# The first feed-forward stage begun on the scale alone, its shift added to four column chunks afterwards

## The chip, the cores and the metric

One core of a Trainium2 chip runs the whole kernel. Five engines work side by side, each through its own queue of instructions in order: TensorE (PE, matmuls and transposes), VectorE (DVE), ScalarE (ACT), GpSimd (POOL, here almost only the issuing of DMAs) and SyncE (SP, DMAs). The metric is the device time of one execution in microseconds (us).

## The reference, cut to what matters

Two layers, 384 tokens (128 of context, 256 latent), width 1024. Only the beginning of layer 0 is touched:

```python
mod = jax.nn.silu(cond) @ p["w_ada"] + p["b_ada"]          # one vector for context, one for latent tokens
mod = mod.reshape(cond.shape[0], N_MOD, 1, D_MODEL)        # (shift, scale, gate) x 3 for each layer
h = rmsnorm(x, g[0]) * (1.0 + mod[:, 1]) + mod[:, 0]       # scale is mod 1, shift is mod 0
x = x + 0.5 * mod[:, 2] * swiglu(h, p["w_ffn_in"][0], p["w_ffn_out"][0])
...                                                       # mixer, then a second such FFN
def swiglu(h, w_in, w_out):
    g, u = jnp.split(h @ w_in, 2, axis=-1)
    return (jax.nn.silu(g) * u) @ w_out
```

With r the factor of the norm for a token, `h @ w_in` is r * ((x * scale') @ w_in) + shift @ w_in, so the shift can be added behind the matmul. The kernel uses that before and after the change.

## The kernel before, in words

Everything is kept with features on the partitions: `xT` is 8 blocks (k = 0 to 7) of 128 features by 384 tokens. Each product is made of three matmuls (`mm3`: wh*xh, wh*xl, wl*xh), for which ACT rounds an operand to its upper part (`wh`, `rH`, `hH`, `aH`) and DVE subtracts it to get the rest (`wl`, `rL`, `hL`, `aL`).

Six stages follow one another: FFN, mixer, FFN for each of two layers. In an FFN the 2816 hidden columns are worked in 22 chunks f; a chunk is 24 matmuls for gate (`pg`) and 24 for up (`pu`), three for each block k, then SiLU, product and split; then 8 output blocks (`po`). The weights of a chunk come in two halves q (k 0 to 3 and 4 to 7), loaded by SP into tiles `X` (5 buffers) and split into `H` and `L` (4 buffers each, so two chunks).

The modulation vectors of 18 groups (stage s; p = shift, scale, gate) are products of `sc` (SiLU of the conditions) with slices of `w_ada`. POOL loads them, 512 KB at a time, into `AX` (3 buffers), and the stream `ada` works them in steps of one block k: on DVE (two instructions over 1024 columns into `accs`, then at the group's end eight matmuls with ones, `adaps`), or on PE (`adaps<-adax,sc`). The numbers in `ADA_F` and `ADA_M` say how many steps stand in each stage.

At the start shift and scale of the first FFN are made apart from that stream: `ada_first(i)`, i = 0 to 3, loads 256 columns of each of the two (four tiles of 512 KB, by SP) and makes 32-row matmuls into one bank, a copy by ACT (`adasb`), a transpose (`psada`) and two small DVE instructions (`md`, `am`). Then `raw_chunk` makes x * scale' for two blocks k, with the shift as two further columns. So the first two chunks of the FFN (`N_RAW`) can start on blocks 0 and 1 while w_ada is still loading. Their banks hold 386 columns, the last two being shift @ w_in, which SiLU and product add. From chunk 2 on the FFN uses `hs`, the fully modulated x (`mod_chunk`).

The order on each engine is made by the framework's scheduler from dependencies and priorities (`ahead`, `placed`); `behind` adds an order without a wait. `late_loads` issues 17 small parameter loads on POOL (among them `gains` and `rot`) once the last `raw_chunk` is done.

Of the kernel before, what the change touches and what calls it, by code (L numbers as in the profile page):

```python
# [84 lines left out]
def hybrid_step_kernel(  # L85
# [104 lines left out]
    mm = nc.tensor.matmul  # L190
    V = nc.vector
# [105 lines left out]
    def ada_first(i):  # L297
# [3 lines left out]
        for q in range(2):  # L301
            xs = []
            for g in range(2):
                if (i + q) % 2 == 0:
                    x = kp.tile([P, HALF_K, 256], F32, name="adax", tag="K")
                else:
                    x = wp.tile([P, HALF_K, 256], F32, name="adax", tag="X")
                rows = w_ada[0, q * HALF_K * P : (q + 1) * HALF_K * P, g * D + 256 * i : g * D + 256 * i + 256]
                nc.sync.dma_start(x, rows.rearrange("(k p) n -> p k n", p=P))
                xs.append(x)  # L310
            for kk in range(HALF_K):
                k = q * HALF_K + kk
                for g in range(2):
                    for j in range(2):
                        r0 = 64 * g + 32 * j
                        mm(
                            bank[r0 : r0 + 32, 0:P],
                            sc[:, k, :],
                            xs[g][:, kk, j * P : (j + 1) * P],
                            start=(k == 0),  # L320
                            stop=(k == KD - 1),
                        )
# [20 lines left out]
    def ada_group(s, p, on_dve):  # L343

        l, i = divmod(s, 3)
# [3 lines left out]
        bias = vC[l][:, i * 24 + KD * p : i * 24 + KD * p + KD]  # L349
        accs = [K5(f"ada{c}") for c in range(2)] if on_dve else None  # L350
        bank = None if on_dve else PS("adaps", "pa")
        for k in range(KD):
            x = wp.tile([P, 1024], F32, name="adax", tag="AX", bufs=3)
            nc.gpsimd.dma_start(x, w_ada[l, k * P : (k + 1) * P, c0 : c0 + D])  # L354
            if on_dve:
                x = x.rearrange("p (h n) -> p h n", h=2)
# [8 lines left out]
            else:  # L365
                x = x.rearrange("p (m a j) -> p a m j", m=KD, a=4)
                for a in range(4):
                    ins = mm(bank[32 * a : 32 * a + 32, 0:256], sc[:, k, :], x[:, a], start=(k == 0), stop=(k == KD - 1))
# [960 lines left out]
    for i in range(4):  # L1329
        ada_first(i)  # L1330
        for k in (2 * i, 2 * i + 1):
            raw_chunk(0, k)
# [61 lines left out]
```

## Time and profile before

| | us |
|---|---|
| median of 3 runs | 1578.61 (1577.85 to 1579.18) |
| the profiled execution, its own time | 1580.6 |
| its span, first to last instruction | 1578.8 |
| first matmul of the first FFN begins | 22.54 |
| its chunk 2 begins (the two raw chunks are done) | 58.58 |
| its output blocks begin | 230.27 |
| first mixer's scores begin | 439.07 |
| second FFN's first matmul | 523.61 |

The times in the stretch are counted from the span's start. In what follows "the start" is the stretch to 58.58 us.

### The profile page before, as it was taken

What the parts mean: (1) busy time and instruction counts of PE and PEld (TensorE: products, weight loads), DVE (VectorE), ACT (ScalarE), POOL (GpSimd) and SP (SyncE); (2) the same over time, 40 slices, a digit from 0 to 9 for tenths busy, and PEclk for the clock granted to TensorE, in tenths of its full rate; (3) what the DMA queues carried; (4) which work ended last, traced back from release to release, by engine and by line L of the source; (5) the groups of instructions that cost most, each with busy time, mean ns of one, the idle gap of its engine ahead of it and who ended that gap; (6) DMA issues with size and microseconds to landing.
All of it is one profiled execution on the core that took longest, in us unless ns stands there. A gap on an engine that the chain in (4) does not pass through costs nothing.

```text
span 1578.8 us, 24260 instructions
## 1 busy us (share of the span) xinstructions
PE 1527.9 (97%) x9118; PEld 1441.2 (91%) x9118; DVE 1113.6 (71%) x2068; ACT 746.6 (47%) x1376; POOL 103.4 (7%) x194
## 2 busy tenths in 40 slices
PE   7999999999889999999999999999978999999998
PEld 5899999998668999999999999999857699999998
DVE  5888586587677988578578866777967789443332
ACT  4533332469577633333363333325975864333221
POOL 1202010001100001001000200110000000000000
PEclk9999999999999999999999999999989999999999
DMA  9978576523531587566537866674231046444341
GB/s 304 248 205 228 158 231 196 147 80 115 185 106 37 146 245 211 161 207 225 171 97 215 238 187 193 203 238 121 64 92 37 15 134 201 130 117 128 116 145 35
DMA packets 291034, 249.02 MB, mean 158 GB/s; under 512 B 11554, under 2 KB 273159, under 8 KB 290917
## 3 DMA queue, kind: packets, MB, share of 16 engines
q1 hardware_dynamic: 270224, 175.94, 38.2%
q0 software_dynamic: 20368, 71.34, 14.8%
q8 instruction: 71, 1.16, 0.3%
q14 instruction: 47, 0.38, 0.1%
q10 hardware_dynamic: 324, 0.20, 0.1%
HBM read 245.17 MB, written 2.27 MB: 157 GB/s over the span
## 4 chain that ended last, share of the span: by engine, by line
PE 88%; DVE 4%; ACT 4%; issue 2%; DMA 1%; POOL 0%; ACTq 0%; DVEq 0%; POOLq 0%
PE po L475 9%; PE po L476 9%; PE po L477 9%; PE pg L475 8%; PE pg L477 8%; PE pg L476 8%; PE pu L475 8%; PE pu L477 8%; PE pu L476 8%; PE psw L476 1%; PE psg L891 1%; PE psw L475 1%; PE psw L477 1%; PE adaps L378 1%; ACT gate L143 1%
## 5 line engine op out<-in xcount | busy, mean ns | idle before, releaser
L471 DVE TENSOR_TENSOR wl<-wx,wh 128x1024 fp32r<-128x1024 f32 (+2 forms) x332 | 385.4, 1163 | 302.8 <-ACT wh L470 294.3
L470 ACT CAST wh<-wx 128x1024 fp32r<-128x1024 f32 (+2 forms) x332 | 333.2, 1005 | 448.5 <-PE po L476 237.3
L362 DVE SCALAR_TENSOR_TENSOR ada<-adax,sc,ada 128x1024 f32<-128x1024 f32 x196 | 244.2, 1280 | 17.8 <-DMA adax<-in_w_ada_dram 17.4
L475 PE MATMUL po<-aH,wh 128*128 128x384 f32 x704 | 239.7, 341 | 0.0
L477 PE MATMUL po<-aH,wl 128*128 128x384 f32 x704 | 237.7, 338 | 0.0
L476 PE MATMUL po<-aL,wh 128*128 128x384 f32 x704 | 237.2, 337 | 0.0
L475 PE MATMUL pg<-hH,wh 128*128 128x384 f32 x640 | 216.9, 339 | 0.0
L475 PE MATMUL pu<-hH,wh 128*128 128x384 f32 x640 | 216.2, 338 | 0.0
L477 PE MATMUL pg<-hH,wl 128*128 128x384 f32 x640 | 215.9, 337 | 0.2 <-DVE wl L471 0.2
L477 PE MATMUL pu<-hH,wl 128*128 128x384 f32 x640 | 215.6, 337 | 0.0
L476 PE MATMUL pu<-hL,wh 128*128 128x384 f32 x640 | 215.5, 337 | 0.0
L476 PE MATMUL pg<-hL,wh 128*128 128x384 f32 x640 | 215.4, 337 | 0.0
L143 ACT ACTIVATE sg<-pg 128x384 f32<-128x384 f32 x80 | 39.4, 493 | 206.5 <-PE pg L477 206.5
L475 PEld LDWEIGHTS po<-aH,wh 128*128 128x128 f32 x704 | 132.4, 188 | 3.9 <-issue 2.1
L476 PEld LDWEIGHTS po<-aL,wh 128*128 128x128 f32 x704 | 132.2, 188 | 0.5 <-issue 0.5
L477 PEld LDWEIGHTS po<-aH,wl 128*128 128x128 f32 x704 | 132.2, 188 | 0.0
L354 POOL DMA_DIRECT2D adax<-in_w_ada_dram x128 | 68.1, 533 | 892.3 <-DVE ada L360 466.5
L475 PEld LDWEIGHTS pg<-hH,wh 128*128 128x128 f32 x640 | 120.2, 188 | 2.5 <-issue 2.1
L477 PEld LDWEIGHTS pg<-hH,wl 128*128 128x128 f32 x640 | 120.1, 188 | 0.6 <-DVE wl L471 0.5
L476 PEld LDWEIGHTS pg<-hL,wh 128*128 128x128 f32 x640 | 120.2, 188 | 0.0
L475 PEld LDWEIGHTS pu<-hH,wh 128*128 128x128 f32 x640 | 120.2, 188 | 0.0
L477 PEld LDWEIGHTS pu<-hH,wl 128*128 128x128 f32 x640 | 120.1, 188 | 0.0
(327 smaller groups left out, 2425.9 us busy)
## 6 DMA issues: line engine op xcount, KB each, us to landing
wx<-in_w_ffn_in_dram SPq DMA_DIRECT2D x352, 256.0 KB, 4.1
adax<-in_w_ada_dram POOLq DMA_DIRECT2D x128, 512.0 KB, 4.9
wx<-in_w_ffn_out_dram SPq DMA_DIRECT2D x80, 512.0 KB, 3.9
wx<-in_w_in_dram SPq DMA_DIRECT2D x28, 512.0 KB, 3.8
adax<-in_w_ada_dram SPq DMA_DIRECT2D x16, 512.0 KB, 7.7
wx<-in_w_ffn_out_dram SPq DMA_DIRECT2D x16, 256.0 KB, 3.3
wx<-in_w_out_dram SPq DMA_DIRECT2D x8, 512.0 KB, 3.9
wx<-in_w_out_dram SPq DMA_DIRECT2D x16, 256.0 KB, 2.7
```

Source lines behind the costliest of these rows:

```text
L143: ins = nc.scalar.activation(out, in_, func, **kw)
L354: nc.gpsimd.dma_start(x, w_ada[l, k * P : (k + 1) * P, c0 : c0 + D])
L362: ins = V.scalar_tensor_tensor(accs[c], x, w, accs[c], ALU.mult, ALU.add)
L378: mm(bank[32 * a : 32 * a + 32, 256 * c : 256 * c + 256], cm(C_ONE, n1=32), x[:, a], start=True, stop=True)
L470: nc.scalar.copy(h[:, 0:nk, 0:ncol], x[:, 0:nk, 0:ncol])
L471: V.tensor_tensor(lo[:, 0:nk, 0:ncol], x[:, 0:nk, 0:ncol], h[:, 0:nk, 0:ncol].bitcast(F32), ALU.subtract)
L475: mm(out, wh, xh, start=first, stop=False)
L476: mm(out, wh, xl, start=False, stop=False)
L477: last_mm[0] = mm(out, wl, xh, start=False, stop=last)
L891: mm(ps[:, 0:TG], wg[:, wi, :], xcs[ch], start=True, stop=True)
```

## The change: what it does

At the start only the scale is loaded and made (`scale_load`, `scale_first`; matmuls of two 32-row groups in place of four). The first four chunks (`N_LATE`) are made from x * scale' alone, 384 columns, and kept as r * gate and r * up in SBUF (`late_acts`). The shift becomes an ordinary group (0, 0) of the stream, worked by PE between and inside chunks 2 and 3, with loads in six buffers (three of `K`, three of `AX`); its first load waits for the last scale matmul. The shift's part of the four chunks is a new group (0, 1): the four chunks' columns of `w_ffn_in` are loaded again by POOL (8 times 512 KB) and multiplied by the shift on DVE, and `late_shift` adds the result, does SiLU, product and split. Chunks 4 and 5 are now the ones with 386 columns. `begin` writes out the order; with `strict` on, every engine keeps the order in which the code is written. `ADA_F[0]` goes from 20 to 28 steps, which begin at chunk 6 instead of 2. The matmuls of the stream are put behind the last `mm3` that is written ahead of them (`last_mm`), before behind the norm's (`norm_last["pe"]`), in the mixers too.

```diff
-ADA_F = [[20, 12], None, [24, 12], [20, 16], None, [8, 0]]
+ADA_F = [[28, 12], None, [24, 12], [20, 16], None, [8, 0]]
+N_LATE = 4
...
+            def run(*a, **k):
+                ins = fn(*a, **k)
+                if strict["on"]:
+                    if self.last is not None:
+                        tc.add_manual_dep(ins.ins, self.last, no_sync, reason="order on the engine")
+                    self.last = ins.ins.name
+                return ins
...
+    TE, SC, V = (InOrder(e) for e in (nc.tensor, nc.scalar, nc.vector))
...
+        late = (s, p) == (0, 1)
+        on_dve = on_dve or late
...
+            if (s, p) == (0, 0) and k % 2 == 0:
+                x = kp.tile([P, 1024], F32, name="adax", tag="K")
+            else:
+                x = wp.tile([P, 1024], F32, name="adax", tag="AX", bufs=3)
+            if late:
+                win = w_ffn_in[0, 0, k * P : (k + 1) * P, :].rearrange("p (g n) -> p g n", g=2)
+                nc.gpsimd.dma_start(x.rearrange("p (g n) -> p g n", g=2), win[:, :, 0 : N_LATE * P])
...
-                    w = sc[:, k, c : c + 1]
+                    w = md[:, k, c : c + 1] if late else sc[:, k, c : c + 1]
...
-                    if norm_last["pe"] is not None:
-                        behind(ins, norm_last["pe"])
+                    behind(ins, last_mm[0])
...
-    ada = Stream([(0, 2)] + [(s, p) for s in range(1, 3 * DEPTH) for p in range(3)])
+    ada = Stream([(s, p) for s in range(3 * DEPTH) for p in range(3)])
...
+        scale_first(2, scales[2])
+        raw_chunk(0, 4)
+        raw_chunk(0, 5)
+        part(1, (2, 3))
+        weights(0, 1)
+        part(0, (4, 5))
+        scale_first(3, scales[3])
+        raw_chunk(0, 6)
+        raw_chunk(0, 7)
+        weights(1, 1)
+        part(1, (4, 5))
+        part(0, (6, 7))
+        keep(0)
+        for q in range(2):
+            weights(2, q)
+        part(1, (6, 7))
+        keep(1)
+        for f in range(2, N_LATE):
+            b.append(banks())
+            hidden(b[f][0:1], {q: sl[f, q] for q in range(2)}, raws[0], T)
+            for q in range(2):
+                weights(f + 1, q)
+            ada.step(2 if f == 2 else 4)
+            if f == 3:
+                for k in range(KD):
+                    raw_cols(0, k)
+            hidden(b[f][1:2], {q: sl[f, q] for q in range(2)}, raws[0], T)
+            if f == 2:
+                ada.step(2)
+            keep(f)
+        strict["on"] = False
+        late_loads(norm_last["raw"])
+        hs = [mod_chunk(0, k, r) for k in range(KD)]
...
-            if f >= 2:
+            f0 = first + 2
+            if f >= f0:
```

How the order moves, in three places (rows as the built programs have them; all operations under the recording layer have line L204 in the changed program).

DVE at the very start, before: copies of the transposed x (`xT<-psx`) and the running sum of squares (`acc<-sq`; the squares are ACT's).

```order
L447 COPY xT_112<-psx_113 128x384
L447 COPY xT_112<-psx_120 128x384
L447 COPY xT_112<-psx_128 128x384
L447 COPY xT_112<-psx_136 128x384
L439 SCALAR_TENSOR_TENSOR acc_118<-sq_125,acc_118 128x384
L447 COPY xT_112<-psx_144 128x384
L439 SCALAR_TENSOR_TENSOR acc_118<-sq_133,acc_118 128x384
```

The same place on DVE in the changed program, from the second copy on:

```order
L204 COPY xT_112<-psx_120 128x384
L204 SCALAR_TENSOR_TENSOR acc_118<-sq_125,acc_118 128x384
L204 COPY xT_112<-psx_128 128x384
L204 SCALAR_TENSOR_TENSOR acc_118<-sq_133,acc_118 128x384
L204 COPY xT_112<-psx_136 128x384
L204 SCALAR_TENSOR_TENSOR acc_118<-sq_141,acc_118 128x384
```

Each sum now stands directly behind the copy of its own block; before, the copies ran three blocks ahead.

ACT around the last scale part of the start, before: the copy `adasb` of that part, the cast of a weight half (`wh`), x * scale' of the last two blocks (`rH`).

```order
L324 COPY adasb_445<-ada0_404 128x128
L470 CAST wh_692<-wx_689 128x1024
L143 ACTIVATE rH_451<-xT_112,am_186 128x128
L143 ACTIVATE rH_451<-xT_112,am_186 128x256
L143 ACTIVATE rH_459<-xT_112,am_186 128x128
L143 ACTIVATE rH_459<-xT_112,am_186 128x256
```

The same place on ACT in the changed program; `wh_431` is the second half of chunk 1, `wh_466` the first of chunk 2:

```order
L204 COPY adasb_413<-ada0_396 64x128
L204 ACTIVATE rH_419<-xT_112,am_209 128x128
L204 ACTIVATE rH_419<-xT_112,am_209 128x256
L204 ACTIVATE rH_425<-xT_112,am_209 128x128
L204 ACTIVATE rH_425<-xT_112,am_209 128x256
L204 CAST wh_431<-wx_201 128x1024
L204 CAST wh_466<-wx_463 128x1024
```

The cast of a weight half stands behind the last blocks' rounding now, not ahead of it.

DVE in chunks 3 to 5 of the changed program: `sg_693`, `su_694` are chunk 3's kept halves, `wl_857`, `wl_864` chunk 5's weights, `wl_937` chunk 6's; `tb` are the first mixer's rotary tables.

```order
L204 TENSOR_TENSOR sg_693<-pg_586,y_316 128x384
L204 TENSOR_TENSOR wl_857<-wx_853,wh_856 128x1024
L204 TENSOR_TENSOR su_694<-pu_587,y_316 128x384
L204 TENSOR_TENSOR wl_864<-wx_860,wh_863 128x1024
L204 TENSOR_SCALAR gains_92<-gains_92 128x2x32
L204 COPY rb_838<-pg_787 128x2
L204 TENSOR_SCALAR gains_92<-gains_92 128x2x96
L204 TENSOR_TENSOR tb_2968<-rot_78,gains_92 128x2x32 x4
L204 TENSOR_TENSOR wl_937<-wx_933,wh_936 128x1024
L204 SCALAR_TENSOR_TENSOR hL_716<-ht_714,md_208,hH_715 128x128
L204 SCALAR_TENSOR_TENSOR hL_716<-ht_714,md_208,hH_715 128x256
L204 COPY rb_840<-pu_788 128x2
```

Before, the first of the same `tb` instructions stands behind the eight steps of the stream's first group:

```order
L362 SCALAR_TENSOR_TENSOR ada0_760<-adax_1346,sc_101,ada0_760 128x1024
L362 SCALAR_TENSOR_TENSOR ada1_761<-adax_1346,sc_101,ada1_761 128x1024
L360 TENSOR_SCALAR ada0_1436<-adax_1438,sc_101 128x1024
L683 TENSOR_TENSOR tb_2931<-rot_78,gains_92 128x2x32
L362 SCALAR_TENSOR_TENSOR ada0_1436<-adax_1513,sc_101,ada0_1436 128x1024
```

The tables, which need the late loads of `gains` and `rot`, moved ahead of chunk 6's weights and of all `hL`.

PE in the first mixer, before, from its last compressed-projection matmul (`psc`) on: the stream's matmuls (`adaps`) stand between the transposes and projections.

```order
L981 MATMUL psc<-wl,hH 128x352
L368 MATMUL adaps<-adax,sc 32x256 x18
L989 MATMUL pst<-kc_76,cl 128x128
L368 MATMUL adaps<-adax,sc 32x256 x2
L989 MATMUL pst<-kc_76,cl 128x128
```

PE later in that mixer in the changed program, behind the first output matmuls (`po`), where the scores (`psS`) and the transposes of probabilities (`psT`) begin:

```order
L204 MATMUL adaps<-adax,sc 32x256 x9
L204 MATMUL psS<-kC,qh 128x384
L204 MATMUL adaps<-adax,sc 32x256 x3
L204 MATMUL psS<-kC,qh 128x384
L204 MATMUL pst<-kc_76,stk 96x128 x32
L204 MATMUL adaps<-adax,sc 32x256 x10
L204 MATMUL psS<-kC,qh 128x384
L204 MATMUL psT<-kc_76,prob 128x128
L204 MATMUL adaps<-adax,sc 32x256 x2
```

All 64 matmuls of the stream's two groups moved from ahead of the scores to between them, 42 of them behind the first `psT`, in 17 small bursts.

## Rows read from the trace of the kernel before

**Rows 1.** The page, part 1: busy time, share of the span, instructions.
```profile
PE 1527.9 (97%) x9118; PEld 1441.2 (91%) x9118; DVE 1113.6 (71%) x2068; ACT 746.6 (47%) x1376; POOL 103.4 (7%) x194
```

**Rows 2.** Timeline of PE at the start: start, length, instruction, idle before.
```profile
9.46 1.91 PE L446 MATMUL psx<-kc,xtok 128*128 128x128 f32 x8
...
17.53 2.76 PE L316 MATMUL ada<-adax,sc 128*32 128x128 f32 x60
...
20.97 0.27 PE L326 MATMUL psada<-kc,adasb 128*128 128x128 f32 x1
...
22.54 0.45 PE L475 MATMUL pg<-rH,wh 128*128 128x386 f32 x1
...
58.58 0.34 PE L475 MATMUL pg<-hH,wh 128*128 128x384 f32 x1
58.76 0.34 PE L476 MATMUL pg<-hL,wh 128*128 128x384 f32 x1
```

**Rows 3.** Timeline of ACT at the start.
```profile
16.25 0.49 ACT L143 ACTIVATE sq<-psx 128x384 f32<-128x384 f32 x1 [2.00 <-DVE xT L447]
...
20.34 0.27 ACT L324 COPY adasb<-ada 128x128 f32<-128x128 f32 x1 [1.26 <-PE ada L316]
20.50 1.05 ACT L470 CAST wh<-wx 128x1024 fp32r<-128x1024 f32 x1
21.68 0.80 ACT L143 ACTIVATE rH<-xT,am 128x128 fp32r<-128x128 f32 x2
22.39 1.03 ACT L470 CAST wh<-wx 128x1024 fp32r<-128x1024 f32 x1
```

**Rows 4.** Timeline of DVE at the start.
```profile
15.60 0.56 DVE L447 COPY xT<-psx 128x384 f32<-128x384 f32 x1 [1.48 <-PE psx L446]
16.08 0.55 DVE L439 SCALAR_TENSOR_TENSOR acc<-sq,acc 128x384 f32<-128x384 f32 x1
...
21.56 0.16 DVE L526 CAST rH<-md 128x2 fp32r<-128x2 f32 x1
...
21.86 1.23 DVE L471 TENSOR_TENSOR wl<-wx,wh 128x1024 fp32r<-128x1024 f32 x1
...
44.14 0.74 DVE L512 SCALAR_TENSOR_TENSOR hL<-ht,md,hH 128x128 fp32r<-128x128 f32 x2
44.80 0.74 DVE L508 SCALAR_TENSOR_TENSOR ht<-xT,am,y 128x128 f32<-128x128 f32 x2
```

**Rows 5.** Busy time by stretch: us, each engine's (instructions), granted clock, DMA.
```profile
40.00:44.00 4.00, 1.62 (x12) 0.78 (x13) 3.80 (x9) 3.45 (x8) 0.00 (x0) 0.89 1.09 347
44.00:50.00 6.00, 6.00 (x42) 4.66 (x43) 2.37 (x9) 0.91 (x2) 0.00 (x0) 0.50 1.19 301
...
398.00:403.00 5.00, 1.60 (x26) 0.68 (x24) 5.00 (x8) 4.71 (x10) 1.57 (x3) 1.00 0.72 228
403.00:408.00 5.00, 3.61 (x20) 1.28 (x21) 2.52 (x9) 1.31 (x5) 1.81 (x4) 0.70 1.04 378
...
453.00:487.00 34.00, 30.70 (x206) 21.38 (x205) 27.63 (x101) 30.07 (x104) 0.00 (x0) 1.00 0.10 32
```

**Rows 6.** Timeline of PE: the stream's matmuls after a DVE group.
```profile
127.01 1.07 PE L378 MATMUL adaps<-ada,kc 128*32 128x256 f32 x16
```

**Rows 7.** Timeline of PE: the stream's matmuls in the first mixer.
```profile
398.10 1.50 PE L368 MATMUL adaps<-adax,sc 128*32 128x256 f32 x24
403.27 0.64 PE L368 MATMUL adaps<-adax,sc 128*32 128x256 f32 x8 [3.67 <-DMA adax<-in_w_ada_dram]
```

**Rows 8.** Timeline of POOL: the first late load and that of `rot`.
```profile
55.47 0.59 POOL L226 DMA_DIRECT2D rowsG<-in_diff_subln_dram  x1 [50.79 <-DVE rL L531]
...
60.31 0.57 POOL L226 DMA_DIRECT2D rot<-in_consts_dram  x1
```

**Rows 9.** The tile `rot`: time of its one load.
```profile
DMA to landing us min/median/max: 6.6/6.6/6.6
```

**Rows 10.** The page, part 5: steps of the stream on DVE.
```profile
L362 DVE SCALAR_TENSOR_TENSOR ada<-adax,sc,ada 128x1024 f32<-128x1024 f32 x196 | 244.2, 1280 | 17.8 <-DMA adax<-in_w_ada_dram 17.4
```

More of the change, by code (lines that the diff above doesn't have):

```diff
@@ L188, in small, with __init__, __getattr__ @@
         return const.tile(list(shape), F32, name=name)
-    mm = nc.tensor.matmul
-    V = nc.vector
+    strict = {"on": False}
+    class InOrder:
+        def __init__(self, engine):
+            self.engine, self.last = engine, None
+        def __getattr__(self, name):
+            fn = getattr(self.engine, name)
+            def run(*a, **k):
[5 more added lines that the diff above has]
+                return ins
+            return run
+    TE, SC, V = (InOrder(e) for e in (nc.tensor, nc.scalar, nc.vector))
+    mm = TE.matmul
     kc0 = small("kc0", (P, 2 * P))
@@ L266, in rows_to_cols @@
         ps = PS("psv", "p1")
-        ins = nc.tensor.transpose(ps[:, 0:n], rows[0:n, :], cm(C_ID, 0, n, 0, n))
+        ins = TE.transpose(ps[:, 0:n], rows[0:n, :], cm(C_ID, 0, n, 0, n))
         if after is not None:
@@ L299, in ada_first, with scale_first @@
+    def scale_first(i, xs):
         md, am = new_mods(0)
         bank = PS("ada0", "pa")
[L301 to L322, printed above, removed]
+        for k in range(KD):
+            for j in range(2):
+                ins = mm(
+                    bank[32 * j : 32 * j + 32, 0:P],
+                    sc[:, k, :],
+                    xs[k // HALF_K][:, k % HALF_K, j * P : (j + 1) * P],
+                    start=(k == 0),
+                    stop=(k == KD - 1),
+                )
+        norm_last["scale"] = ins
@@ L352, in ada_group @@
         for k in range(KD):
-            x = wp.tile([P, 1024], F32, name="adax", tag="AX", bufs=3)
-            nc.gpsimd.dma_start(x, w_ada[l, k * P : (k + 1) * P, c0 : c0 + D])
+            if (s, p) == (0, 0) and k % 2 == 0:
+                x = kp.tile([P, 1024], F32, name="adax", tag="K")
+            else:
+                x = wp.tile([P, 1024], F32, name="adax", tag="AX", bufs=3)
+            if late:
+                win = w_ffn_in[0, 0, k * P : (k + 1) * P, :].rearrange("p (g n) -> p g n", g=2)
+                nc.gpsimd.dma_start(x.rearrange("p (g n) -> p g n", g=2), win[:, :, 0 : N_LATE * P])
+            else:
+                ins = nc.gpsimd.dma_start(x, w_ada[l, k * P : (k + 1) * P, c0 : c0 + D])
+                if (s, p) == (0, 0):
+                    if k == 0:
+                        tc.add_manual_dep(ins.ins, norm_last["scale"].ins.name, sync, reason="order of the loads")
+                        first_load.append(ins)
+                    else:
+                        behind(ins, first_load[0])
             if on_dve:
@@ L562, in ffn, with late_shift @@
+    late_acts = []
+    def late_shift(b):
+        for f in range(N_LATE):
+            sg, su_ = late_acts[f]
+            for j, sl in SEG:
+                act(sg[:, sl], sg[:, sl], AF.Silu, bias=b[:, j, 0, f, 0:1])
+            for j, sl in SEG:
+                V.scalar_tensor_tensor(sg[:, sl], su_[:, sl], b[:, j, 1, f, 0:1], sg[:, sl], ALU.add, ALU.mult)
+            late_acts[f] = split(sg, "a", pool=LT)
     def ffn(s, r, hs, last, ready=None):
@@ L797, in cache_prep @@
         pt = PS("pst", "p2")
-        nc.tensor.transpose(pt[:, 0:P], cck[:, 0:P], ident)
+        TE.transpose(pt[:, 0:P], cck[:, 0:P], ident)
         cn = S("cn", (P, P))
-        nc.scalar.copy(cn, pt[:, 0:P])
+        SC.copy(cn, pt[:, 0:P])
         ps = PS("psk", "p2")
@@ L1326, in hybrid_step_kernel @@
     NS = 3 * DEPTH
-    r = norm_stat(0)
-    ready = {0: [], 1: []}
[L1329 to L1332, printed above, removed]
-        if i in (0, 2):
-            for f in range(2):
-                ready[f].append(ffn_slab(0, f, i // 2))
-    hs = [mod_chunk(0, k, r) for k in range(KD)]
-    late_loads(norm_last["raw"])
+    r, hs, ready = begin()
     state_out = small("state_out", (P, 16))
```

182 lines of the change are left out of this document (123 added, 59 removed).

## The prediction

> **What bounds the kernel now.** I read the page first: PE is busy 97% of the span [rows 1], so a change can only bring time where PE waits or works on something that can go. Then the timeline of PE at the start: the first FFN matmul is at 22.54, chunk 2 begins at 58.58, and from there the pitch of a matmul is 58.76 - 58.58 = 0.18 us [rows 2]. Two chunks have 96 matmuls, 96 x 0.176 = 16.9 us; they take 36 us. So the start has some 19 us beside FFN work, and the stretches show where: from 40 to 44 PE is busy 1.62 of 4 us, and from 44 to 50 its granted clock is 0.50, the lower of its two levels (1.2 in place of 2.4 GHz) [rows 5]. That is what the change can attack. From 58.58 on there is next to nothing to win before the first mixer, where PE waits 3.67 us for a stream load [rows 7].
>
> **Start up to chunk 2, worked out along the new order.** Eight of the sixteen first w_ada loads go, 4.2 MB, at the 347 GB/s of [rows 5] 12 us of loading; then the chains between the engines decide.
>
> First the norm's squares. On ACT a square starts only after DVE's copy of its block: copy 15.60 to 16.16, square at 16.25 to 16.74 [rows 3, 4]. The new DVE order puts the sum of a block behind the copy of the same block, so copy, square and sum follow one another: 0.56 + 0.09 + 0.49 + 0.05 + 0.47 (pitch of copy and sum, 16.08 - 15.60 = 0.48) = 1.65 us for each of blocks 2 to 5. The first copy can start near 10.2 (the transposes run from 9.46 at 0.21 us each [rows 2]), block 2 at 12.3, block 5 at 17.3, the last copy ends near 19.9, the last square at 20.5. The scale's copy `adasb` stands behind it on ACT: 20.5, against 20.34 before [rows 3]. Nothing is gained up to here, though PE could be ready at 17.3.
>
> From a copy `adasb` at S, its transpose ends at S + 0.9 and rounding `rH` starts at S + 1.34 (20.97 + 0.27 and 21.68 against 20.34); two blocks of `rH` cost 2 x 0.71 (22.39 - 21.68), a cast 0.95 to 1.05, then `wl` 1.2 [rows 2 to 4]. Followed through the order as written: part 0 at S = 20.5, first FFN matmuls near 24.2 (the second scale copy waits on ACT for cast and `rH` of the first), chunk 0 blocks 0 to 3 until 28.5, the norm's sums 2.3, chunk 1 blocks 0 and 1 until 32.9, scale matmuls 1.5 (32 at 46 ns, from 60 in 2.76 [rows 2]), copy at 34.5, chunk 1 blocks 2 and 3 from 35.5 to 37.6. Then chunk 0 needs its second half, whose cast stands on ACT behind `rH` of blocks 4 and 5 (38.4) and whose `wl` ends at 39.6: PE idles 0.8 twice and ends at 41.4. Last scale part: matmuls to 43.0, `adasb` 43.05, `rH` 44.4 to 45.8, cast to 46.9, `wl` to 48.1. PE has nothing else in between (3.9 us less one transpose), then 10 + 24 matmuls: chunk 2 begins at **54.1**, against 58.58.
>
> This is at full clock. Before, the clock fell after a stretch in which PE was busy 1.62 of 4 us, and 6 us ran at 0.50, 3 us lost; in the mixer a wait of 3.67 us cost 0.30 of 5 us, 1.5 us [rows 5, 7]. The new start has two such stretches: 17.3 to 24.2 (some 2.1 us of work in 7) and 41.4 to 48.1 (some 2). I take 1.8 us for each, nearer the mixer's case: chunk 2 at 57.7, **-0.9 us**. Bounds: no loss (-4.5) and 3 us twice (+1.5).
>
> The Trainium skill, "TensorE: Matmul & The Clock Gate", section on the HAM clock gate, says that the throttled state is the default and activity releases it, so that idling is paid for a second time after it. By that both stretches are paid; by the trace's rows alone one could doubt the second, and the sum would be 1.8 us lower. The trace agrees where it shows the case (granted 0.50 behind the stretch with 1.62 of 4).
>
> **The shift on PE.** 32 matmuls of the program, 64 records of 256 columns, in three bursts of 16, 16 and 32 inside chunks 2 and 3, which had none before. A burst of 16 takes 1.07, one of 24 takes 1.50 [rows 6, 7], so 32 take 1.9: **+4.0 us** (bounds 3.5, if the burst's own ends overlap, and 5). The six buffers hide the loads: the first six are issued near 43 and needed from 58 on; the last two are issued at the first burst and needed 11 us later.
>
> **The late group.** 16 steps' instructions more on DVE, 16 x 1.28 = 20.5 us [rows 10], and at its end 16 records on PE, **+1.1 us** [rows 6]. Its matmuls with ones wait for DVE, bounds 1 to 2. The 0.2 us that PE waited at 59 go: **-0.2**.
>
> **Chunk 6.** Let chunk 2 begin at C. PE's order gives chunk 3's middle at C + 14.7, the shift's last burst until C + 16.6, then DVE transposes, adds (0.7, an estimate from the small rows) and writes eight pairs of columns at 0.30 (21.56 to 21.86 [rows 4]): C + 19.7. Only then the first late load is issued. Before, `rot` was issued 60.31 - 55.47 = 4.8 us after the first one and landed 6.6 us later [rows 8, 9], so it lands at C + 31.3 (bounds 30, if it lands faster with less traffic, and 34.5, if the three 512 KB loads now ahead of it in POOL's queue hold it up). DVE has `tb`, which needs `rot`, in front of chunk 6's first `wl` and of all `hL`. What is queued behind it: 4 x 0.22, `wl` 1.15, six blocks of `hL` and five of `ht` at 0.66 each (44.80 - 44.14 [rows 4]), and one read of 0.48 that empties chunk 4's gate bank, which chunk 6 writes: 9.8 us, C + 41.1; then two more `hL`, one read and the second `wl`, 3 us. PE is there at C + 4 x 8.4 + 4.1 = C + 37.7. It waits 3.4 us for the bank and about 1 more for the second `wl`: **+4.3 us** (2 to 7.5). What is late next is DVE, which is at chunk 6's end some 3 us behind and has it back by chunk 8.
>
> **DVE from chunk 6 to 21.** 28 steps in 16 chunks, before 20 in 20. A chunk: two `wl` 2.3, product and split 0.95, 3.5 step instructions at 1.2, 4.3: 7.5 of 8.4 us, with the late shift's 4 x 1.1 and the small parameters in single chunks. Weights are prepared a chunk ahead, so single chunks over 8.4 pass: **+0.5** (0 to 10).
>
> **The first mixer.** Its 64 stream matmuls go from the gaps ahead of the scores into the stretch of scores. Won: the wait of 3.67 and the clock's 1.5, up to 5.2 us, but the wait is mostly a wait for ACT and DVE that would be there anyhow (in 398 to 403 DVE is busy 5.00 and ACT 4.71 of 5 [rows 5]); I take 2.5. Paid: 17 bursts, by 0.25 + 0.05 us for each record (from 8 in 0.64 and 24 in 1.50), 17 x 0.25 + 84 x 0.05 = 8.4 us, in a stretch of 34 us where PE is busy 30.70 and ACT 30.07 [rows 5]. About half fits into PE's small gaps: 4.5. Together **+2** (-5 to +8).
>
> **Sum.** -0.9 + 4.0 + 1.1 - 0.2 + 4.3 + 0.5 + 2 = **+10.8 us**. Behind the first mixer the order hardly moves. The profiled execution took 1580.6, 2.0 over the median, and its span 1578.8; the sum moves either alike, so 1578.6 + 10.8 = **1589.4**.
>
> **Rivals.**
> - *The start runs at PE's own pace* (faster). If squares and casts keep out of the way, PE goes on at 17.3: 16.9 of FFN, three more scale parts 4.5, transposes 1.2, sums 2.3, chunk 2 near 42.2, 15.5 us less than I have. Total -4.7, 1574. For it: DVE and ACT are far from full up to 40 us. Against: the order is fixed, and the chain of squares is a row. It decides if chunk 2 begins before 43.7. Chance 0.17.
> - *The mixer gives back what the start costs* (no change). All 5.2 us are won and the bursts fit into the gaps: -5.2 in place of +2, and with the wait at chunk 6 at its lower bound, 2, the total is +1.3: 1580. Chance 0.15.
> - *DVE becomes the bound from chunk 6 on*: 28 steps plus waits for loads (17.8 us over 196 steps now [rows 10]) put each chunk near 8.9: +8, in all 1598. Chance 0.13.
> - *The shift comes too late for chunk 3*: the last two loads, issued at the first burst, miss the third one, as stream loads did in the mixer by 3.67; +4, and `rot` moves with it: 1595. Chance 0.07.
> - The forecast: 0.48.
>
> A measurement of this kernel tells 0.2%, 3.2 us. Faster takes the first rival and little else, 0.18; same 0.15; slower 0.67. The range from 1574 to 1598 takes the first rival's time and the DVE bound's, and leaves 0.2 outside. The forecast's own range is 1583 to 1596.
>
> **What would show it.** In the changed profile: first `adasb` within 0.5 of 20.5; first FFN matmul near 24; a PE gap of 3 to 4 us near 43 ended by ACT's cast; a granted clock below 0.8 near 24 to 28 and 47 to 51; chunk 2 (third `pg` bank) near 57.7; three bursts of `adaps` within chunks 2 and 3; DVE waiting on a DMA ahead of `tb` for 5 us or more, and PE waiting at chunk 6 for DVE; output blocks near 240 against 230.27; the first mixer 2 us longer. Wrong it would be if chunk 2 began before 50, if `tb` did not wait, or if the mixer became shorter by more than 4.

## The result, and the profile after

The changed kernel takes **1597.67 us** (median of 4 runs, 1593.39 to 1600.71), beside 1578.24 us for the kernel before (4 runs): ratio 1.012 [1.009, 1.0151], slower by some 19 us. The profiled execution took 1600.71 with a span of 1598.9; the one before had 1580.6 and 1578.8. The direction of the forecast held and its wide range, 1574 to 1598, by 0.3 us only; its own range, 1583 to 1596, was missed, and its size, +10.8, is 8 to 9 us too small.

| profiled execution, us | before | after | difference | forecast |
|---|---|---|---|---|
| chunk 2 begins | 58.58 | 59.10 | +0.5 | -0.9 |
| from there to the output blocks | 171.69 | 181.39 | +9.7 | +9.7 |
| output blocks | 97.60 | 97.77 | +0.2 | 0 |
| first mixer, from its first projection to the second FFN's first matmul | 195.73 | 203.51 | **+7.8** | **+2** |
| everything behind | 1055.2 | 1057.1 | +2.0 | 0 |

The page: PE is busy 11 us longer than in [rows 1], in 48 instructions fewer.

```profile
PE 1538.9 (96%) x9070; PEld 1451.3 (91%) x9070; DVE 1136.8 (71%) x2099; ACT 746.0 (47%) x1380; POOL 113.2 (7%) x210
```

PE at the start (start, length, idle before and what ended it):

```profile
19.64 0.37 PE L204 MATMUL psada<-kc,adasb 64*128 64x64 f32 x1 [3.13 <-ACT adasb L204]
19.94 3.63 PE L204 MATMUL ada<-adax,sc 128*32 128x128 f32 x32
...
24.27 0.69 PE L204 MATMUL pg<-rH,wh 128*128 128x384 f32 x1
...
40.34 0.44 PE L204 MATMUL pg<-rH,wh 128*128 128x384 f32 x1 [0.63 <-ACT wh L204]
...
41.60 0.45 PE L204 MATMUL pg<-rH,wl 128*128 128x384 f32 x1 [0.64 <-DVE wl L204]
...
49.09 0.44 PE L204 MATMUL pg<-rH,wh 128*128 128x384 f32 x1 [2.91 <-ACT wh L204]
...
50.34 0.69 PE L204 MATMUL pg<-rH,wl 128*128 128x384 f32 x1 [0.60 <-DVE wl L204]
...
59.10 0.33 PE L204 MATMUL pg<-rH,wh 128*128 128x384 f32 x1
```

Where a matmul has 0.69 us in place of 0.44, the clock is at its lower level (granted 0.50 from 20 to 28 us and from 50 to 56 us). The first scale copy on ACT stands behind the chain of squares, which go at a pitch of 1.6 us:

```profile
11.97 0.49 ACT L204 ACTIVATE sq<-psx 128x384 f32<-128x384 f32 x1 [1.09 <-DVE xT L204]
13.56 0.49 ACT L204 ACTIVATE sq<-psx 128x384 f32<-128x384 f32 x1 [1.09 <-DVE xT L204]
...
19.34 0.25 ACT L204 COPY adasb<-ada 64x128 f32<-64x128 f32 x1
```

The windows of two stretches of the start, columns as in [rows 5] (the granted clock is the third number from the right):

```profile
24.00:34.00 10.00, 10.00 (x39) 9.08 (x40) 3.14 (x8) 3.44 (x7) 0.00 (x0) 0.75 0.91 241
44.00:54.00 10.00, 6.08 (x42) 5.31 (x39) 3.08 (x7) 4.58 (x8) 3.28 (x6) 0.78 0.76 278
```

The shift's three bursts on PE (16 records take 1.07 us, as in [rows 6]):

```profile
63.38 1.07 PE L204 MATMUL adaps<-adax,sc 128*32 128x256 f32 x16
68.79 1.07 PE L204 MATMUL adaps<-adax,sc 128*32 128x256 f32 x16
74.19 1.93 PE L204 MATMUL adaps<-adax,sc 128*32 128x256 f32 x32
```

DVE ahead of chunk 6, and PE at that chunk's first matmul:

```profile
88.20 0.20 DVE L204 TENSOR_SCALAR gains<-gains 128x64 f32<-128x64 f32 x1 [5.50 <-DMA gains<-in_diff_qk_norm_dram]
...
90.31 0.63 DVE L204 TENSOR_TENSOR tb<-rot,gains 128x64 f32<-128x64 f32 x4 [0.68 <-DMA rot<-in_consts_dram]
90.86 1.22 DVE L204 TENSOR_TENSOR wl<-wx,wh 128x1024 fp32r<-128x1024 f32 x1
...
99.36 0.55 DVE L204 TENSOR_TENSOR sg<-pg,y 128x384 f32<-128x384 f32 x1
```

```profile
100.06 0.41 PE L204 MATMUL pg<-hH,wh 128*128 128x384 f32 x1 [2.55 <-ACT hH L204]
```

The trace names ACT's `hH` as the releaser of PE. DVE's read of chunk 4's gate bank ends at 99.36 + 0.55 = 99.91, just as late, and is the read that frees the bank; which of the two ended the wait is not shown, but ACT's `hH` itself is made from DVE's `ht`.

The first mixer in windows: the wait behind the compressed projections with PE idle, then the projections behind it, at a lower clock.

```profile
408.50:415.00 6.50, 0.02 (x1) 0.02 (x1) 5.94 (x13) 4.99 (x12) 0.00 (x0) 0.72 0.55 163
415.00:428.00 13.00, 10.97 (x28) 5.99 (x29) 7.50 (x22) 4.01 (x12) 1.49 (x3) 0.76 0.09 29
```

Its stream matmuls, the first and two of the smallest of 20 bursts. All now stand behind the first scores (449.18); those of [rows 7] stood ahead of them:

```profile
461.19 1.48 PE L204 MATMUL adaps<-adax,sc 128*32 128x256 f32 x18
...
473.67 0.62 PE L204 MATMUL adaps<-adax,sc 128*32 128x256 f32 x2
...
475.84 0.62 PE L204 MATMUL adaps<-adax,sc 128*32 128x256 f32 x2
```

### The profile page after: what moved, and what is told of

Its sections match the earlier page's. It is cut to its first block, busy times and chain, and to the rows that moved or that the text cites. A ratio compares the mean times of both kernels' runs of the same rounds, so it can differ in the third digit from the quotient of the medians.

```text
span 1598.9 us, 24217 instructions
## 1 busy us (share of the span) xinstructions
PE 1538.9 (96%) x9070; PEld 1451.3 (91%) x9070; DVE 1136.8 (71%) x2099; ACT 746.0 (47%) x1380; POOL 113.2 (7%) x210
## 4 chain that ended last, share of the span: by engine, by line
PE 86%; DVE 4%; issue 3%; ACT 3%; DMA 1%; POOL 0%; DVEq 0%; POOLq 0%; ACTq 0%
PE po L204 27%; PE pg L204 23%; PE pu L204 23%; PE psw L204 3%; PE adaps L204 2%; PE psO L204 1%; PE psg L204 1%; DVE hscan L204 1%; ACT gate L204 1%; PE psS L204 1%; PE psa L204 1%; PE psT L204 1%; ACT L204 1%; PE psn L204 1%; PE pst L204 1%
## 5 line engine op out<-in xcount | busy, mean ns | idle before, releaser
L204 DVE TENSOR_TENSOR wl<-wx,wh 128x1024 fp32r<-128x1024 f32 (+2 forms) x332 | 384.9, 1162 | 269.3 <-ACT wh L204 257.8
L204 ACT CAST wh<-wx 128x1024 fp32r<-128x1024 f32 (+2 forms) x332 | 332.1, 1002 | 467.3 <-PE po L204 229.3
L204 DVE SCALAR_TENSOR_TENSOR ada<-adax,sc,ada 128x1024 f32<-128x1024 f32 x196 | 244.4, 1281 | 16.1 <-DMA adax<-in_w_ada_dram 15.4
L204 PE MATMUL po<-aH,wh 128*128 128x384 f32 x704 | 239.8, 341 | 0.0
L204 PE MATMUL po<-aH,wl 128*128 128x384 f32 x704 | 238.0, 338 | 0.0
L204 PE MATMUL po<-aL,wh 128*128 128x384 f32 x704 | 237.2, 337 | 0.0
L204 PE MATMUL pg<-hH,wh 128*128 128x384 f32 x608 | 206.6, 340 | 2.6 <-ACT hH L204 2.6
L204 PE MATMUL pg<-hH,wl 128*128 128x384 f32 x608 | 205.7, 338 | 0.0
L204 PE MATMUL pg<-hL,wh 128*128 128x384 f32 x608 | 205.4, 338 | 0.0
L204 PE MATMUL pu<-hH,wh 128*128 128x384 f32 x608 | 205.1, 337 | 0.0
L204 PE MATMUL pu<-hH,wl 128*128 128x384 f32 x608 | 205.0, 337 | 0.0
L204 PE MATMUL pu<-hL,wh 128*128 128x384 f32 x608 | 204.7, 337 | 0.0
L204 PEld LDWEIGHTS po<-aH,wh 128*128 128x128 f32 x704 | 132.5, 188 | 3.9 <-issue 2.1
L204 PEld LDWEIGHTS po<-aL,wh 128*128 128x128 f32 x704 | 132.3, 188 | 0.5 <-issue 0.5
L204 PEld LDWEIGHTS po<-aH,wl 128*128 128x128 f32 x704 | 132.2, 188 | 0.0
L204 ACT ACTIVATE sg<-pg 128x384 f32<-128x384 f32 x76 | 37.3, 491 | 198.9 <-PE pg L204 198.9
L204 PEld LDWEIGHTS pg<-hH,wh 128*128 128x128 f32 x608 | 114.5, 188 | 5.7 <-ACT hH L204 2.8
L204 PEld LDWEIGHTS pg<-hL,wh 128*128 128x128 f32 x608 | 114.7, 189 | 0.0
L204 PEld LDWEIGHTS pg<-hH,wl 128*128 128x128 f32 x608 | 114.6, 188 | 0.0
L204 PEld LDWEIGHTS pu<-hH,wh 128*128 128x128 f32 x608 | 114.2, 188 | 0.0
L204 PEld LDWEIGHTS pu<-hL,wh 128*128 128x128 f32 x608 | 114.2, 188 | 0.0
```

The costliest lines, as they stand in the source:

```text
L204: ins = fn(*a, **k)
```

## The experiments

Theory: two things are larger than forecast, the mixer, which pays for all of the moved matmuls and wins nothing, and the clock. Rivals: DVE's 28 steps, a backlog of DVE or loads that the new beginning leaves behind, waits with no clock in them. Each kernel was run several times beside the kernel before (1579.3 to 1580.6 in those sets). A stage is read from the one profiled execution.

| | us, median (range, runs) | ratio to before | chunk 2 begins | to output blocks | first mixer | second mixer |
|---|---|---|---|---|---|---|
| before (first profile) | | | 58.58 | 171.69 | 195.73 | 193.53 |
| changed (first profile) | | | 59.10 | 181.39 | 203.51 | 195.93 |
| e11 changed, again | 1599.01 (1593.31 to 1600.84, 5) | 1.0115 [1.0098, 1.0133] | 55.50 | 181.53 | 203.75 | 194.21 |
| e1 mixer order back | 1585.36 (1584.75 to 1590.80, 6) | 1.0041 [1.0025, 1.0057] | 55.08 | 179.89 | 194.75 | 193.46 |
| e2 before, new order | 1590.31 (1589.68 to 1592.03, 6) | 1.0067 [1.0053, 1.008] | 58.28 | 171.70 | 204.65 | 195.83 |
| e3 tables held | 1592.92 (1591.68 to 1594.84, 6) | 1.0084 [1.0069, 1.0099] | 54.92 | 177.01 | 203.14 | 195.54 |
| e4 squares free | 1594.57 (1591.58 to 1595.20, 6) | 1.0088 [1.0074, 1.0103] | 53.85 | 181.01 | 203.81 | 195.74 |
| e5 casts early | 1587.28 (1587.10 to 1588.30, 5) | 1.005 [1.0038, 1.0063] | 47.85 | 180.95 | 203.47 | 194.17 |
| e6 all four | **1574.44** (1572.66 to 1575.60, 5) | **0.9966** [0.9953, 0.998] | 45.35 | 177.01 | 196.21 | 193.83 |
| e7 no late group | 1597.83 (1596.28 to 1601.17, 4) | 1.0118 [1.0102, 1.0135] | 57.92 | 179.61 | 204.13 | 196.71 |
| e8 idle filled | 1592.20 (1590.05 to 1595.81, 6) | 1.0083 [1.0068, 1.0098] | 56.53 | 180.88 | 200.83 | 190.99 |
| e9 all four, stream in second mixer | 1573.43 (1572.08 to 1578.40, 9) | 0.9966 [0.9955, 0.9977] | 45.75 | 176.99 | 196.67 | 199.21 |
| e10 before, stream in second mixer | 1582.05 (1579.07 to 1586.71, 12) | 1.0014 [1.0003, 1.0025] | 57.48 | 171.70 | 196.77 | 196.77 |
| e12 all four, idle filled | **1571.47** (1568.37 to 1573.73, 6) | **0.9951** [0.9937, 0.9964] | 46.20 | 177.01 | 196.82 | 190.92 |

**e1, the mixer's order.**

```diff
-                    behind(ins, last_mm[0])
+                    behind(ins, norm_last["pe"])
...
```

> The changed kernel, with the stream's matmuls on PE put behind the norm's last matmul again, as before. Measured so far from the first mixer's first projection to the second FFN's first matmul: 195.7 us before, 203.5 in the changed kernel. Theory (the order of these 64 matmuls is what the mixer pays for: 8 us of bursts between the scores, and a wait of 6.50 us that they no longer fill): this stretch is 196 us again, the total falls by 7 to 8.5 us against the changed kernel, to about 1590. Rival (the mixer is longer because it comes with other loads and another DVE backlog behind it, the order hardly matters): the stretch stays above 201 us and the total falls by less than 3 us.

The stretch is 194.75 and the total 12 us lower than the changed kernel's 1597.67: more than expected, with the start 4.0 us shorter than in the first profile (55.08), though nothing there was edited. PE in its wait, into which the stream puts 24 + 8 + 4 records almost for nothing (from the first projection to the first scores it takes 111.8 us, 110.9 in the changed kernel):

```profile
402.89 1.50 PE L204 MATMUL adaps<-adax,sc 128*32 128x256 f32 x24
...
408.03 0.64 PE L204 MATMUL adaps<-adax,sc 128*32 128x256 f32 x8 [3.64 <-DMA adax<-in_w_ada_dram]
409.28 1.07 PE L204 MATMUL adaps<-adax,sc 128*32 128x256 f32 x4 [0.61 <-DMA adax<-in_w_ada_dram]
410.28 0.47 PE L204 MATMUL pst<-kc,cl 128*128 128x128 f32 x1
```

**e2, the same order in the kernel before.**

```diff
-                    if norm_last["pe"] is not None:
-                        behind(ins, norm_last["pe"])
+                    behind(ins, last_mm[0])
```

> The kernel before, with one edit: the stream's matmuls on PE are put behind the last mm3 written ahead of them. Theory (the order alone costs it): the first mixer's stretch grows from 195.7 to 203.5 us and the total by 7 to 8.5 us, to about 1586. Rival (it needs the new beginning): within 3 us of before.

204.65 us, and 9.7 us over before in all (1590.31 against 1580.58), more than expected; in its profile the second mixer is 2.3 us longer too. The order alone lengthens the first mixer, without the new beginning. The rival of a backlog is out.

**e3, the tables.**

```diff
-                V.tensor_tensor(
+                ins = V.tensor_tensor(
                     tb[:, kind, :, o + 32 : o + 64].rearrange("p t (a d) -> p t a d", a=2),
...
+                behind(ins, hold["dve"])
...
-            V.tensor_scalar(gains[:, :, g0 : g0 + n], gains[:, :, g0 : g0 + n], float(n) ** -0.5, None, op0=ALU.mult)
+            ins = V.tensor_scalar(gains[:, :, g0 : g0 + n], gains[:, :, g0 : g0 + n], float(n) ** -0.5, None, op0=ALU.mult)
+            behind(ins, norm_last["dve"])
```

> The changed kernel, with the rotary tables and the scaling of the gains put behind all hL on DVE, so that DVE does not stop at them for a DMA. Theory (DVE's stop at the tables delays chunk 6): chunk 6 starts without PE waiting, its matmuls run at full clock; chunk 2 to the output blocks falls from 181.4 to 177 us, the total by 4 to 5 us, to about 1593. Rival (DVE is behind at chunk 6 anyway, for the hL of all eight blocks are made there): chunk 6 still waits 2 us or more and the total falls by less than 2.

177.01 us as expected. DVE no longer meets a DMA, and chunk 6's first matmul follows without a gap:

```profile
83.67 1.23 DVE L204 TENSOR_TENSOR wl<-wx,wh 128x1024 fp32r<-128x1024 f32 x1 [2.87 <-ACT wh L204]
```

```profile
93.01 0.34 PE L204 MATMUL pu<-rH,wl 128*128 128x386 f32 x1
93.18 0.34 PE L204 MATMUL pg<-hH,wh 128*128 128x384 f32 x1
```

**e4, the squares.** The fixed order begins behind the transposes.

```diff
-    strict["on"] = True
     for k in range(KD):
```

> The changed kernel, with the fixed order beginning only behind the transposes of x, so that the copies of x run ahead of the sums of squares again. Theory (the chain copy, square, sum holds the first scale copy on ACT back): first adasb near 16.8 us in place of 19.3, first FFN matmul near 21 in place of 24.3, PE waits less than 1.5 us ahead of it, so its clock stays up there; chunk 2 begins 3.5 to 5.5 us earlier, the total is 1592 to 1594. Rival (the first scale part is held by its loads, as the part before the change was): adasb moves by less than 0.5 us and nothing changes.

On ACT the copy now stands ahead of the last two squares, and waits for PE:

```profile
17.62 0.26 ACT L204 COPY adasb<-ada 64x128 f32<-64x128 f32 x1 [3.68 <-PE ada L204]
```

The first FFN matmul is at 21.37 and the clock is 1.00 from 14 to 34 us. The median falls by 3.1, a little less than expected; chunk 2, at 53.85, is 5.2 us ahead of the first profile, 1.1 to 4.1 ahead of the other profiles with that beginning (54.92 to 57.92).

**e5, the casts.**

```diff
         part(1, (0, 1))
+        weights(0, 1)
         scale_first(2, scales[2])
...
-        weights(0, 1)
+        weights(1, 1)
         part(0, (4, 5))
...
         raw_chunk(0, 7)
-        weights(1, 1)
```

> The changed kernel, with the casts and rests of the second weight halves of chunks 0 and 1 written ahead of the scale parts 2 and 3, so that on ACT they stand ahead of the rounding of blocks 4, 5 and 6, 7. Theory (PE's waits of 0.63, 0.64, 2.91 and 0.60 us near 40 and 49 are for these casts, and the lower clock near 50 is what the wait costs on top): these four waits are gone, chunk 2 begins at 49 to 51 us (55.0 and 54.9 in two runs with the same beginning, 59.1 in the first profile), the total falls by 4 to 7 us against the changed kernel, to 1590 to 1593. Rival (the last scale part's own chain of copy, transpose, modulation and rounding is as long, so PE waits for it instead): a wait of 2 us or more stays near 46 and chunk 2 begins after 53.

All four waits are gone, chunk 2 begins at 47.85, earlier than expected, and the total falls by 10.4, where 4 to 7 were expected. The waits themselves are 0.63 + 0.64 + 2.91 + 0.60 = 4.8 us; the clock that followed them goes too (compare 0.78 above):

```profile
34.00:44.00 10.00, 9.28 (x72) 8.62 (x73) 6.12 (x18) 4.99 (x12) 2.84 (x6) 1.00 0.50 138
44.00:54.00 10.00, 10.00 (x69) 9.17 (x68) 7.14 (x9) 3.44 (x4) 1.32 (x3) 1.00 1.07 378
```

**e6, the four edits together.**

> The changed kernel with four edits together: the stream's matmuls behind the norm's, the rotary tables behind all hL, the fixed order only behind the transposes of x, the casts of the second halves early. Theory (four separate losses): they add up, 10 + 4.8 + 3 + 5 = some 23 us less than the changed kernel's 1597.7, so 1573 to 1578, and faster than the kernel before (1580.6 on this chip) by 3 to 8 us. Rival (with one wait gone the next thing is late: DVE with the hL at chunk 6, or the loads at the start): the gains overlap, the time is 1580 to 1585 and not faster than before.

1574.44, as expected, and the kernel is 0.34% faster than before. That the four add up is not shown to the microsecond: the falls of the four single medians, 12.3, 4.8, 3.1 and 10.4, sum to 30.5 us, that of all four is 23.2. A likely reason, not shown, is that the changed kernel has two times (see the last section) and a median takes one or the other. By lowest times it is 18.5 and 20.7. The rival, 1580 to 1585, is out. Chunk 2 begins 13.2 us earlier than before; 5.3 of that go to shift and late group.

**e7, no late group.** The shift's part of four chunks is left out.

```diff
-ADA_F = [[28, 12], None, [24, 12], [20, 16], None, [8, 0]]
+ADA_F = [[20, 12], None, [24, 12], [20, 16], None, [8, 0]]
...
-                act(sg[:, sl], sg[:, sl], AF.Silu, bias=b[:, j, 0, f, 0:1])
+            act(sg, sg, AF.Silu)
...
```

> The changed kernel without the late group: the shift's part of the four first chunks is left out (no reloading of the columns, no 16 instructions on DVE, no 16 matmuls with ones, SiLU without a bias), 20 in place of 28 steps in the first FFN. Theory (DVE has room; the group costs PE its 16 matmuls and little else): chunk 2 to the output blocks falls from 181.4 by 1.1 to 2.5 us, the total by 1 to 3. Rival (DVE bounds chunks 6 to 21 with 28 steps): it falls by 6 to 8 us.

The stage falls by 1.8 us, as the theory has it; the median does not move, where 1 to 3 us were expected (such a difference is within the spread of both). The fall of 6 to 8 us of a DVE bound is not there.

**e8, the wait filled.**

```diff
...
+        for i in range(36):
+            ins = nc.tensor.matmul(dum[:, 0:T], hs[0][0][:, 0:P], hs[0][0], start=True, stop=True)
+            behind(ins, fin_c)
...
         cl = norm_c(l, pc)
```

> The changed kernel with 36 useless matmuls (128x384, one operand pair, into a bank of which two columns are copied) on PE in each mixer between its last compressed-projection matmul and the transposes of cl, where PE is idle for 6.50 us. Theory (behind an idle wait the clock runs at the lower level, and that is paid in the projections behind it: 6.5 us for six psk matmuls): the granted clock stays 1.00 from there to the scores, the first mixer's stretch falls from 203.5 to 199 or 200 us, the second's from 195.9 to 192, the total by 6 to 9 us. Rival (the clock is not what the stretch waits for, ACT and DVE are): no change beyond 2 us, or slower because the useless work runs over.

The clock stays at 1.00, and the same 28 or 29 PE instructions behind the wait take 10.70 us where they took 13.00; the gain is less than expected for the first mixer (200.83 us) and more for the second (190.99); the total falls by 5.5.

```profile
405.20:411.70 6.50, 6.42 (x38) 6.10 (x36) 6.10 (x12) 5.00 (x11) 0.00 (x0) 1.00 0.54 173
411.70:422.40 10.70, 8.48 (x29) 4.44 (x30) 6.29 (x19) 4.02 (x13) 1.50 (x3) 1.00 0.11 35
```

The Trainium skill, "TensorE: Matmul & The Clock Gate", section "HAM oscillation — how this bites in real kernels", advises to restructure a loop whose matmuls wait for DMA between its pieces, so that PE stays at its higher clock. These rows agree that an idle wait costs clock: even useless work pays, 2.7 us in the first mixer and 3 to 5 in the second (190.99 beside 194.21 and 195.93 in the two profiles of the changed kernel).

**e9 and e10, useful work in that place.** Of the fourth stage's 16 steps beside its output blocks, eight go to the second mixer and eight into the stage's chunks. The edit is e9's, on the four of e6; e10 makes the same one in the kernel before, whose first number is 20.

```diff
-ADA_F = [[28, 12], None, [24, 12], [20, 16], None, [8, 0]]
-ADA_M = [14, 0]
+ADA_F = [[28, 12], None, [24, 12], [28, 0], None, [8, 0]]
+ADA_M = [14, 8]
```

> All four edits, and eight steps of the stream (64 records on PE) moved from the fourth stage's DVE to the second mixer, where by the order they stand among the compressed projections and in the 6.50 us behind them. Theory (that wait can take work for nothing, and the clock behind it stays up): the second mixer's stretch falls from 193.8 to 191 us as with the useless matmuls, the fourth stage loses one DVE group's 16 matmuls with ones, 1.07 us; together 3 to 4 us less than all four alone (1574.4), so 1570.5 to 1572. Rival (the eight loads of the stream come late and the matmuls wait for them in that place, as one did by 3.67 us in the first mixer): no change within 1 us, or up to 3 us slower.

> The kernel before, with the same eight steps moved to the second mixer and nothing else. Theory: the same 3 to 4 us less, 193.5 to 191 us in the second mixer, 1575.5 to 1577.5 in all where before has 1579 to 1580.6 on this chip. Rival: as for the kernel with the four edits.

The theory fell, and the rival holds. Nothing to speak of is gained in e9 (1573.43 against 1574.44; its profiled execution, with 199.21 in the second mixer, was the longest of nine), and e10 is 1.7 us slower than before. Ahead of the scores the second mixer is 1.9 us longer in e9 than in e6 and 2.1 longer in e10 than before; the rest of the 199.21 lies behind them. The records stand in the wait, but the later ones wait there for their loads; the clock falls all the same, and the transposes of `cl` come 1.4 us later in e9 than in e6. PE and two windows of e9:

```profile
1159.21 1.50 PE L204 MATMUL adaps<-adax,sc 128*32 128x256 f32 x24
1164.88 1.08 PE L204 MATMUL adaps<-adax,sc 128*32 128x256 f32 x8 [4.17 <-DMA adax<-in_w_ada_dram]
```

```profile
1159.00:1167.00 8.00, 3.56 (x38) 1.06 (x36) 7.18 (x15) 6.11 (x16) 2.28 (x5) 0.80 0.85 299
1167.00:1175.00 8.00, 8.00 (x29) 4.55 (x27) 2.24 (x7) 2.80 (x7) 1.46 (x3) 0.78 0.69 240
```

**e11, the changed kernel again.**

> The changed kernel once more, unedited, to have it beside the others. Theory (its two times, near 1594 and 1600.7, come from the clock at the start, since chunk 2 began at 59.1 in its first profile and at 54.9 to 57.9 in four experiments that have the very same beginning): times from 1593 to 1601, median 1594 to 1598, and a profile whose chunk 2 begins early has the shorter span by as much. Rival: one of the two times was a disturbance of that chip, and all times now lie within 2 us of 1594.

The two times are there again (1593.31 and 1595.76; 1599.01 to 1600.84). The profiled one took 1595.76 with chunk 2 at 55.50; its span is 4.9 us below the first profile's, 3.6 of it in the start and 1.7 in the second mixer.

**e12, the four edits with the second mixer's wait filled.** 

```diff
...
+        if l == 1:
+            dum = PS("dum", next(turn))
+            for i in range(36):
+                ins = nc.tensor.matmul(dum[:, 0:T], hs[0][0][:, 0:P], hs[0][0], start=True, stop=True)
+                behind(ins, fin_c)
...
```

> The changed kernel with the four edits, and in the second mixer alone the 36 useless matmuls of the earlier run in PE's wait of 6.5 us. In the two kernels with eight steps of the stream moved there, the same wait was taken by 36 records of the stream over 8.0 us, and the clock fell behind it as before. Theory (what counts is that PE works without a break in the wait; the stream's matmuls wait for their loads in it): the granted clock is 1.00 from the wait to the scores, the second mixer's stretch is 191 us in place of 193.8, the total 1571 to 1573. Rival (the gain of the useless matmuls was one of the chances of the clock elsewhere in that run): 193 us or more, and 1574 to 1576 as with the four edits alone.

190.92 us (193.83 in e6) and 1571.47 in all, 0.49% faster than before: the lowest median here, though the intervals of e6 and e12 overlap. PE and the windows:

```profile
1160.91 6.43 PE L1137 MATMUL dum<-hH 128*128 128x384 f32 x36
1167.57 1.65 PE L204 MATMUL pst<-kc,cl 128*128 128x128 f32 x9 [0.23 <-ACT cl L204]
```

```profile
1161.00:1167.50 6.50, 6.33 (x37) 6.01 (x35) 5.99 (x12) 5.01 (x12) 0.00 (x0) 1.00 0.52 164
1167.50:1178.00 10.50, 8.40 (x28) 4.36 (x29) 6.21 (x19) 3.90 (x13) 1.08 (x2) 1.00 0.13 39
```

## Why the prediction was right in direction and too small

**The start (-0.9; measured +0.5, and -3.1 in e11) was right in its mechanism.** First `adasb` 19.34 (forecast 20.5 within 0.5, so this sign failed; the copies of x began at 8.78 us, not at 10.2), first FFN matmul 24.27 (24.2), a wait of 2.91 for the cast (3 to 4 forecast), chunk 2 at 59.10 (57.7). That 24.27 fits is luck: the 32 scale matmuls ahead of it, priced at 1.5 us, took 3.63 at the lower clock, and in e11, where they took 1.94, it is 22.50. The clock's price, 2 x 1.8, was the weak term: by full clock chunk 2 would be at 54.1, and six profiles of this one beginning have it between 54.92 and 59.10. e4 and e5 show the two causes, the squares and the order of cast and rounding.

**The shift (+4.0) measured +4.4**: chunks 2 and 3 take 10.68 and 10.58 where 8.42 is usual. **The late group (+1.1)** measured 1.1 in its chunk (9.52 for 8.43); e7 gives 1.8 with all that hangs on it.

**Chunk 6 (+4.3) measured +4.4, by the forecast wait and by a term that it had not**: from chunk 5's first matmul to chunk 6's it is 11.21 us, from there to chunk 7's 10.02, where 8.43 is usual, and the output blocks begin at 240.49 (240). DVE waited 5.50, 0.90 and 0.68 us for `gains` and `rot`, as forecast, and e3 takes 4.4 out of the stage by moving those instructions alone. PE's wait is 2.55 us (3.4 forecast). The "about 1 more for the second `wl`" is not there: PE does not wait again before chunk 7, and chunk 6's 1.6 us over the usual are mostly the clock, 0.83 from 100 to 110 us. In e1, with the same order, the clock stays at 1.00 there and chunk 6 takes 8.71. So the close fit is in part luck. (A slip of the prediction: 19.7 + 4.8 + 6.6 is 31.1, not 31.3; the first `tb` stood at 31.2 behind chunk 2's beginning.) **DVE (+0.5)** was right to within what can be seen.

**The first mixer (+2) is the step that failed, in size: +7.8.** In e11's profile, 15.2 us longer than before, it is the only stage far from the forecast (+8.0; start -3.1, up to the output blocks +9.8, behind the mixer +0.2). Two parts of the step were wrong. "Won: the wait of 3.67 and the clock's 1.5 ... I take 2.5": nothing was won. From the first projection to the first scores it takes 110.9 us now and 111.2 before, for PE's wait is one for ACT and DVE and lasts 6.50 us with nothing in it, and the clock falls behind it with the stream in it (0.70 in [rows 5]) or without (0.76 in the windows above). The second mixer of the kernel before, which has no stream matmuls in that place, had shown that, and I did not read it there:

```profile
1173.64 0.79 PE L989 MATMUL pst<-kc,cl 128*128 128x128 f32 x2 [6.50 <-ACT cl L143]
```

"Paid: 8.4 us ... about half fits into PE's small gaps": behind the first scores stand 128 records in 20 bursts, 13.0 us from their starts to the next start, where before there were 36 in 4, 3.4 us (a matmul of the program is two records here, so 46 of the 64 matmuls moved behind the scores, not all). That is 9.6 us more, near the 8.4 that I had for the 17 small bursts, and the stretch from the scores to the second FFN is 8.1 us longer, 92.6 for 84.5. So 1.5 us fit into gaps, not half: 0 won and 8.1 paid stand against 2.5 and 4.5. e1 and e2 show the whole of it to be the order.

**Behind the mixer (0; measured +2.0).** 2.4 us are the second mixer, whose instructions on PE stand as before; in ten of the profiles that same order takes from 193.46 to 196.71 us. 1.6 of them arise between 1275 and 1288 us, where the granted clock of that execution goes down to 0.83 (1270 to 1280); e11, the same kernel, has no such drop. The other 0.8 arise between the projections `psk` and the scores. The extra 1.6 us or more are in five of the eight profiles with the first mixer's new order (first profile, e2, e3, e4, e7) and in none of four with the old one (before, e1, e6, e12); whether the order brings the drop is not shown, and why it comes in one execution and not in the next is open.

**The rivals.** The DVE bound falls by e7 (1.8 us where it would have given 6 to 8), the shift that comes too late by the third burst (32 records in 1.93 us, no wait). The mixer that gives back is the contrary of what happened. PE's own pace at the start was not reached; most of it was there to be had: e6 begins chunk 2 at 45.35, where I had put that case at 42.2. That 1597.67 lies inside the wide range is luck: its upper end, 1598, was the time of the DVE bound, which is not what made the kernel slow. Left open: whether the shift's 4.4 us could be had for less; moving it off PE was not tried.

## What to carry to other kernels

Where a bound engine waits, low-priority work that sits in the wait can cost next to nothing (in the first mixer less than 1 us, 8.1 where it went). So before moving it, look for a stage where the same wait stands empty (here the second mixer), to see whether the wait goes away with it, and count what the work costs where it goes. On an engine with a fixed order, read at each small instruction what it waits for and what stands behind it: the tables, which the first mixer reads more than 300 us later, cost 4.4 us, and two casts written behind a rounding 7 or more. Here a wait on TensorE often cost itself and then some of the clock; work that needs no late load kept the clock up through it, the stream's matmuls, which wait for loads, did not.

## What the runs showed of the hardware

**One program, two times.** The nine executions of the changed kernel took 1593 to 1596 or 1599 to 1601 us. At its start the order is the same in the first profile and e1, e3, e7, e8, e11, yet chunk 2 begins at 59.10, 55.08, 54.92, 57.92, 56.53 and 55.50, and what differs is the granted clock. From the first FFN matmul to chunk 2 PE's idle time is 5.2 to 5.6 us in all six; the clock is 0.75 from 24 to 34 us in the first profile (above), and in e3:

```profile
24.00:34.00 10.00, 10.00 (x72) 8.96 (x74) 5.58 (x14) 3.45 (x7) 0.00 (x0) 1.00 0.88 238
```

The Trainium skill, "TensorE: Matmul & The Clock Gate", section "What's actually happening", says that the number of slow matmuls of one kernel varies from run to run. The rows agree; here the start differs by up to 4.2 us.

**Half-filled waits.** Behind a wait in which PE was busy 3.56 of 8 us the granted clock was 0.78; behind the one filled without a break (6.33 of 6.50) 1.00.

**Small bursts.** 2 records of the stream take 0.62 us, 8 take 0.64, 18 take 1.48, 32 take 1.93: most of a small burst's time is the burst's own, not its records'.
